# A later planned landing for all four query tiles of the opening attention head

## The chip, the core and the metric

The kernel runs on one core of a Trainium2 chip. The metric is the device time of one execution in microseconds, lower is better. The kernel before takes 1893.55 us, the median of three runs (1892.68 to 1895.55).

## The reference

One layer of a streaming encoder. A prompt of 2048 frames and a sample of 64 frames with 4096 cached frames go through the same layer:

```python
h = rmsnorm(x, norm_g) @ w_in          # 1024 -> 6144 columns: qa ka va za qb kb vb zb ga gb
# branch A: differential attention, 4 heads, two 64-wide halves c of q and k, values 128 wide
s = einsum('bqhcd,bkhcd->bhcqk', q, k) * 64 ** -0.5 - slope[h] * abs(q_pos - k_pos)
s = where(k_pos // 64 <= q_pos // 64, s, -inf)
p = softmax(s);  a = p[:, :, 0] - lam * p[:, :, 1];  oa = einsum('bhqk,bkhe->bqhe', a, v)
# branch B: retention, 4 heads, 128-wide keys and values, a decayed state over chunks of 64
# output: x + (sigmoid(ga) * ((rms(oa) * silu(za)) @ w_oa) + sigmoid(gb) * ((rms(ob) * silu(zb)) @ w_ob)) @ w_out
```

It returns both outputs, the normalised keys, the values and the final retention states.

## The kernel before, in words

All products are made in pairs of rounded operands: a high part (`wh`, `xh`, `ath`) and the low rest (`wl`, `xl`, `atl`), and each product takes three matmuls. The projection is streamed in two halves of 1024 frames. Its weights come in slabs of 128 rows of `w_in`: SP loads a slab into `ws` (line 266, three buffers), ACT rounds it to `wh` (line 993), GpSimd subtracts to get `wl` (line 1003), and TensorE uses it (line 1039, tile `mm`). A group of 512 columns needs eight slabs. The value columns of the second half are such a group: one tile of 128 frames takes 24 matmuls of 512 columns, slab by slab, and its result is taken out by ACT as `thi` (line 1287, a single buffer) and `raw` (line 1289), by DVE as `tlo` (line 1291), and stored by SP (line 271).

Attention of the first 1024 frames runs while the projection of the second half goes on. A head has four query tiles, p = 0 to 3, of 256 frames each, here numbered within the half. `load_head` (line 1472) loads a head's keys `K` and values `V`, `load_q` (line 1509) loads a query tile with four transfers of 128 KB into one of two buffers `q`. `attn_head` (line 1550) takes the tiles in turn: for each of a tile's two blocks of 128 queries and each half c it makes scores (lines 1582 and 1583, into banks `s` or `tp`), DVE takes them out with the distance term (line 1591), ACT takes the exponential (line 1622), DVE mixes the two halves (line 1644), TensorE transposes the result (line 1694, tile `at`), ACT and DVE split it into `ath` (line 1708) and `atl` (line 1710), and TensorE multiplies by the values (lines 1672 to 1674, tile `pv`).

Nothing of this order is decided on the chip. A planner in Python runs generators as tasks, keeps an estimated clock for each engine (`self.pe`, `self.act` and so on), and writes down instructions in the order in which the tasks come due. Each engine and SP's queue then work through their own list strictly in order, held by semaphores. A task that yields a time is not resumed before the planner's TensorE clock has reached it; until then tasks of lower rank, above all the projection, put their matmuls into the list. `load_q` puts each tile with the time `t` at which the planner takes it to have landed into the list `self.qs`, and `attn_head` yields that time (`yield tq`) before the tile's scores. So a later `t` puts more projection matmuls ahead of these scores in TensorE's list; it adds no wait to the program. `FIRSTQ` is 4000 of the planner's nanoseconds, and in the kernel before it is added to the first tile (line 1494) alone:

```python
        q, tq = self.qs.pop(0)
        yield tq
```

Of the kernel before, what the change touches and what calls it, by code (L numbers as in the profile page):

```python
# [44 lines left out]
FIRSTQ = 4000.0  # L45
# [118 lines left out]
class Hybrid:  # L164
# [1307 lines left out]
    def load_head(self, half, h):  # L1472
        ap = self.ap
        nu = half + 1
        ks = [[None] * nu for _ in range(2)]
        vs = [[None] * nu for _ in range(2)]
        tk = tv = 0
        for u in range(nu):
            usl = slice(1024 * u, 1024 * u + 1024)
            for c in range(2):  # L1480
                yield from self.take("K")
                k = self.sb(ap, [128, 1024], "K", dt=F32R)
                for j in range(2):
                    o = 64 * (j ^ c)
                    tk = self.ld(k[o:o + 64].bitcast(F32), self.kT[j][h, 64 * c:64 * c + 64, usl], 1 << 18)
                ks[c][u] = k
        hd = {"ks": ks, "vs": vs, "tk": tk, "tv": None}
        if self.far:
            self.heads.append(hd)
        else:  # L1490
            self.far = True
            yield from self.load_q(0, 0)
            q, t = self.qs[0]
            self.qs[0] = q, t + FIRSTQ
            yield self.pe + 3000
            yield from self.load_q(0, 1)
            yield self.pe + 2000
            self.ld(self.dfar, self.i["c_dfar"], 1 << 19)
            self.heads.append(hd)
        for u in range(nu):  # L1500
            usl = slice(1024 * u, 1024 * u + 1024)
            for j in range(2):
                yield from self.take("V")
                v = self.sb(ap, [128, 8, 128], "V", dt=F32R)
                tv = self.ld(v.bitcast(F32), self.vN[j][usl, 128 * h:128 * h + 128]
                             .rearrange("(t p) e -> p t e", p=128), 1 << 19)
                vs[j][u] = v
        hd["tv"] = tv

    def load_q(self, h, p):  # L1510
        t0 = 256 * p
        yield from self.take("q")
        q = self.sb(self.ap, [128, 4, 256], "q", dt=F32R)
        for j in range(2):
            qj = self.qT[j][h, :, t0:t0 + 256].rearrange("(c d) t -> d c t", c=2)
            for o in (0, 64):
                t = self.ld(q[o:o + 64, 2 * j:2 * j + 2].bitcast(F32), qj, 1 << 17)
        self.qs.append((q, t))

    def q_loader(self, half):  # L1520
        for h in range(4):
# [1373 lines left out]
```

## Time and profile before

| | us |
|---|---|
| median of the three runs | 1893.55 |
| the profiled execution | 1897.48 |
| its span, first to last instruction | 1895.5 |
| TensorE busy in the span (share 99%) | 1877.3 |
| VectorE busy (67%) | 1267.2 |
| ScalarE busy (50%) | 955.9 |

The profiled execution took 1897.48 us, 1.98 us more than its span, and lies 3.93 us above the median. TensorE is busy for all but 18.2 us of the span, so the time is the sum of its work and of the few places where it stands still. The share of an engine says how much of the span it worked; where TensorE stands still, the view of waits and the order of time show what ended the pause. Starts are given in microseconds from the start of the span.

### The profile page before, as it was taken

The numbers are of one execution on the slowest core, as the hardware profiler recorded it, in microseconds if no ns is written. First come the engines' busy times: TensorE is split into PE (matmuls) and PEld (weight loads), VectorE is DVE, ScalarE is ACT, GpSimd is POOL, SyncE is SP. The second block draws the span as 40 slices with busy tenths as digits, with TensorE's granted clock in tenths as the row PEclk, the third lists the DMA queues.
The fourth block names the chain that finished last, engine by engine and source line by source line (L and its number), as shares of the span: only waits on it lengthen the run. The fifth ranks groups of instructions, "written<-read, shape, count | busy, mean of one in ns | idle before, by whom it ended". The sixth has DMA issues, their size and how long they took to land.

```text
span 1895.5 us, 32109 instructions
## 1 busy us (share of the span) xinstructions
PE 1877.3 (99%) x10970; PEld 1649.7 (87%) x10970; DVE 1267.2 (67%) x2994; ACT 955.9 (50%) x2217; POOL 590.8 (31%) x557
## 2 busy tenths in 40 slices
PE   9999999999999899999999999999999999999999
PEld 7788888888888789888888899999999999999887
DVE  6765856657575667877577776687873329977664
ACT  6434654454434566455556555566664436654221
POOL 2420356555643132031211112211113526522442
PEclk9999999999999999999999999999999999999999
DMA  7654555565566785565523444734414748876542
GB/s 255 213 175 124 169 169 165 168 193 180 179 181 187 222 233 157 143 204 135 160 73 105 137 120 119 203 85 116 116 52 127 227 133 261 269 237 205 174 157 77
DMA packets 360581, 313.01 MB, mean 165 GB/s; under 512 B 67937, under 2 KB 310241, under 8 KB 360418
## 3 DMA queue, kind: packets, MB, share of 16 engines
q1 hardware_dynamic: 360418, 310.97, 56.0%
q8 instruction: 86, 1.41, 0.3%
q14 instruction: 77, 0.63, 0.1%
HBM read 205.43 MB, written 104.60 MB: 164 GB/s over the span
## 4 chain that ended last, share of the span: by engine, by line
PE 65%; DMA 2%; SPq 1%; DVE 1%; ACT 0%; issue 0%; POOL 0%; DVEq 0%; POOLq 0%; ACTq 0%
PE mm L1039 26%; PE at L1694 3%; PE s L1582 2%; PE s L1583 2%; PE pv L1674 2%; PE pv L1673 2%; PE pv L1672 2%; PE s L2496 1%; PE s L2498 1%; PE s L2497 1%; PE mm L2372 1%; PE at L2373 1%; PE s L2372 1%; PE s L2373 1%; PE at L2372 1%; PE s L2374 1%
## 5 line engine op out<-in xcount | busy, mean ns | idle before, releaser
L1003 POOL TENSOR_TENSOR wl<-ws,wh 128x512 fp32r<-128x512 f32 x125 | 172.5, 1396 | 360.5 <-ACT wh L993 271.8
L1039 PE MATMUL mm<-xh,wh 128*128 128x256 f32 (+2 forms) x784 | 258.4, 330 | 0.0
L1039 PE MATMUL mm<-xh,wl 128*128 128x256 f32 (+2 forms) x784 | 254.4, 324 | 0.0
L1039 PE MATMUL mm<-xl,wh 128*128 128x256 f32 (+2 forms) x784 | 254.2, 324 | 0.0
L1039 PE MATMUL mm<-wh,xh 128*128 128x512 f32 x504 | 203.3, 403 | 0.0
L1039 PE MATMUL mm<-wh,xl 128*128 128x512 f32 x504 | 197.8, 392 | 0.0
L1039 PE MATMUL mm<-wl,xh 128*128 128x512 f32 x504 | 197.6, 392 | 0.0
L1622 ACT ACTIVATE row<-row,a_mx 128x1024 f32<-128x1024 f32 (+7 forms) x144 | 149.6, 1041 | 16.4 <-DVE a_mx L1601 16.4
L1039 PEld LDWEIGHTS mm<-xh,wl 128*128 128x128 f32 x784 | 148.1, 189 | 10.3 <-POOL wl L1003 0.5
L1039 PEld LDWEIGHTS mm<-xh,wh 128*128 128x128 f32 x784 | 148.2, 189 | 9.9
L1039 PEld LDWEIGHTS mm<-xl,wh 128*128 128x128 f32 x784 | 148.4, 189 | 9.6
L1710 DVE TENSOR_TENSOR atl<-at,ath 128x512 fp32r<-128x512 f32 (+1 forms) x144 | 92.5, 659 | 80.4 <-ACT ath L1708 80.0
L1448 POOL TENSOR_TENSOR r_y<-r_y,r_sq 128x256 f32<-128x256 f32 x32 | 27.7, 865 | 360.1 <-DVE r_sq L1445 193.3
L1708 ACT CAST ath<-at 128x512 fp32r<-128x512 f32 (+1 forms) x144 | 79.4, 565 | 105.8 <-PE at L1694 103.5
L1591 DVE CUSTOM_DVE_ANT_0 row<-s,dfar 128x512 f32<-128x512 f32 (+2 forms) x150 | 93.2, 635 | 52.5 <-PE s L1583 47.6
L768 POOL TENSOR_TENSOR wl<-ws,wh 128x256 fp32r<-128x256 f32 x64 | 57.5, 899 | 190.7 <-ACT wh L759 187.1
L1039 PEld LDWEIGHTS mm<-wh,xl 128*128 128x128 f32 x504 | 94.7, 188 | 21.3
L1039 PEld LDWEIGHTS mm<-wh,xh 128*128 128x128 f32 x504 | 94.8, 188 | 17.4 <-DVE tlo L1291 0.2
L1039 PEld LDWEIGHTS mm<-wl,xh 128*128 128x128 f32 x504 | 95.0, 188 | 17.0
L1644 DVE SCALAR_TENSOR_TENSOR row<-row,a_w 128x1024 f32<-128x1024 f32 (+5 forms) x88 | 98.9, 1131 | 0.0
L993 ACT CAST wh<-ws 128x512 fp32r<-128x512 f32 x128 | 76.9, 621 | 38.6 <-DMA ws<-in_w_in_dram 25.8
L1582 PE MATMUL s<-K,q 128*128 128x512 f32 (+3 forms) x244 | 93.2, 384 | 1.3 <-DVE a_acc L1591 1.0
(497 smaller groups left out, 5441.3 us busy)
## 6 DMA issues: line engine op xcount, KB each, us to landing
ws<-in_w_in_dram SPq DMA_DIRECT2D x160, 256.0 KB, 3.5
q<-qT SPq DMA_DIRECT2D x128, 128.0 KB, 3.7
K<-kT SPq DMA_DIRECT2D x48, 256.0 KB, 4.3
V<-vN SPq DMA_DIRECT2D x24, 512.0 KB, 5.2
row<-in_x_prompt_dram SPq DMA_DIRECT2D x16, 512.0 KB, 4.4
wz<-in_w_in_dram SPq DMA_DIRECT2D x32, 256.0 KB, 4.3
row<-in_cache_k_T_dram SPq DMA_DIRECT2D x32, 256.0 KB, 3.5
row<-in_cache_v_diff_dram SPq DMA_DIRECT2D x32, 256.0 KB, 3.1
```

Of the source, the lines that this page charges most:

```text
L768: nc.gpsimd.tensor_sub(l[:, cs], src, h[:, cs].bitcast(F32))
L993: self.nc.scalar.copy(h, st)
L1003: self.nc.gpsimd.tensor_sub(l, st, h.bitcast(F32))
L1039: nc.tensor.matmul(ps, p, q, start=c == 0 and i == 0, stop=c == KC - 1 and i == 2)
L1582: nc.tensor.matmul(ps, q1s, kk, start=True, stop=False)
L1591: nc.vector.tensor_tensor_reduce(out=row[:, k0:k0 + n], in0=ps, in1=tab, scale=-SLOPES[h], scalar=3.0e38, op0=ALU.add, op1=ALU.min, accum_ ...
L1622: nc.scalar.activation(u, u, AF.Exp, bias=mx, scale=-1.0, accum_out=lp[:, k:k + 1])
L1644: nc.vector.scalar_tensor_tensor(out=u0, in0=u1, scalar=w[:, 0:1], in1=u0, op0=ALU.mult, op1=ALU.add)
L1694: nc.tensor.transpose(at[:, w:w + 128], src, self.ident)
L1708: nc.scalar.copy(ah[:, :w], at[:, :w])
L1710: nc.vector.tensor_sub(al[:, :w], at[:, :w], ah[:, :w].bitcast(F32))
L2372: nc.tensor.matmul(ps, wh[:, u, csl], oh, start=kt == 0, stop=False)
```

## The change

`FIRSTQ` is no longer added to the first tile after it has been loaded, but by `load_q` to every tile of head 0 with p up to 3, which are the four tiles of the first half's first head:

```diff
@@ -1490,8 +1490,6 @@
         else:
             self.far = True
             yield from self.load_q(0, 0)
-            q, t = self.qs[0]
-            self.qs[0] = q, t + FIRSTQ
             yield self.pe + 3000
             yield from self.load_q(0, 1)
             yield self.pe + 2000
@@ -1515,7 +1513,7 @@
             qj = self.qT[j][h, :, t0:t0 + 256].rearrange("(c d) t -> d c t", c=2)
             for o in (0, 64):
                 t = self.ld(q[o:o + 64, 2 * j:2 * j + 2].bitcast(F32), qj, 1 << 17)
-        self.qs.append((q, t))
+        self.qs.append((q, t if h or p > 3 else t + FIRSTQ))
```

No instruction is added or taken away; the lists are put in another order from the second query tile on. Lines of the changed kernel after 1494 are numbered two lower (1580 for 1582).

On TensorE, where the second query tile's scores (`q_6284`) begin. Before:

```order
L1583 MATMUL s_6411<-K_6243,q_6246 128x256
L1582 MATMUL s_6418<-K_6240,q_6284 128x384
L1583 MATMUL s_6418<-K_6240,q_6284 128x384
L1582 MATMUL tp_6435<-K_6243,q_6284 128x384
L1583 MATMUL tp_6435<-K_6243,q_6284 128x384
```

and in the changed kernel:

```order
L1581 MATMUL s_6411<-K_6243,q_6246 128x256
L1039 MATMUL mm_6364<-xh1_6086,wh_5993 128x320
L1039 MATMUL mm_6364<-xl1_6087,wh_5993 128x320
L1039 MATMUL mm_6364<-xh1_6086,wl_5994 128x320
L1039 MATMUL mm_6364<-xh1_6086,wh_5993 128x320
L1039 MATMUL mm_6364<-xl1_6087,wh_5993 128x320
L1039 MATMUL mm_6364<-xh1_6086,wl_5994 128x320
L1039 MATMUL mm_6443<-wh_6017,xh0_6021 128x512
L1039 MATMUL mm_6443<-wl_6018,xh0_6021 128x512
L1039 MATMUL mm_6443<-wh_6017,xl0_6022 128x512
L1580 MATMUL s_6453<-K_6240,q_6284 128x384
```

Nine projection matmuls now stand between the first tile's last score and the second tile's first.

Still on TensorE, where the third query tile (`q_6428`, in the changed kernel `q_6426`) begins, in the first frame tile of the value columns (`mm_6476`, now `mm_6443`). Before, with five of the eight slabs used:

```order
L1039 MATMUL mm_6476<-wh_6374,xh0_6021 128x512
L1039 MATMUL mm_6476<-wl_6375,xh0_6021 128x512
L1039 MATMUL mm_6476<-wh_6374,xl0_6022 128x512
L1582 MATMUL tp_6511<-K_6240,q_6428 128x256
L1583 MATMUL tp_6511<-K_6240,q_6428 128x256
L1582 MATMUL s_6515<-K_6240,q_6428 128x384
```

and in the changed kernel, the sixth slab to the eighth and the start of the next frame tile; three transposes and six more projection matmuls lie between the last row shown here and the third query tile:

```order
L1039 MATMUL mm_6443<-wh_6385,xh0_6021 128x512
L1039 MATMUL mm_6443<-wl_6386,xh0_6021 128x512
L1039 MATMUL mm_6443<-wh_6385,xl0_6022 128x512
L1039 MATMUL mm_6443<-wh_6422,xh0_6021 128x512
L1039 MATMUL mm_6443<-wl_6423,xh0_6021 128x512
L1039 MATMUL mm_6443<-wh_6422,xl0_6022 128x512
L1039 MATMUL mm_6443<-wh_6449,xh0_6021 128x512
L1039 MATMUL mm_6443<-wl_6450,xh0_6021 128x512
L1039 MATMUL mm_6443<-wh_6449,xl0_6022 128x512
L1039 MATMUL mm_6533<-wh_6017,xh0_6021 128x512
L1039 MATMUL mm_6533<-wl_6018,xh0_6021 128x512
L1039 MATMUL mm_6533<-wh_6017,xl0_6022 128x512
```

The first frame tile's last slab (`wh_6449`, before `wh_6482`) used to come after the third query tile's first six score matmuls and now comes ahead of them; the third query tile stands behind 18 more projection matmuls and three transposes.

On ACT, around the second frame tile's result (`thi_6667`, now `thi_6660`) and the second query tile's transposed result (`ath_6678`, now `ath_6671`). Before:

```order
L1622 ACTIVATE row_6222,a_lp_6638<-row_6222,a_mx_6590 128x768
L1287 CAST thi_6667<-mm_6593 128x512
L1289 COPY raw_6666<-mm_6593 128x512
L1708 CAST ath_6678<-at_6673 128x512
L1708 CAST ath_6686<-at_6682 128x384
```

and in the changed kernel:

```order
L1620 ACTIVATE row_6222,a_lp_6635<-row_6222,a_mx_6613 128x640
L1287 CAST thi_6660<-mm_6533 128x512
L1289 COPY raw_6659<-mm_6533 128x512
L1706 CAST ath_6671<-at_6666 128x512
L1706 CAST ath_6679<-at_6675 128x384
```

The two casts of the attention result stand behind the value result's cast in both; one exponential has moved behind them. On SP's queue the loads and stores from the first query tile's load to the second frame tile's value stores come in one order in both kernels, apart from two small stores that go one place ahead, past one weight load. Five loads later the two orders part.

## The prediction

> **What bounds the kernel now.** I read the page first: does one engine set the time, and how long does it stand still?
>
> ```profile
> span 1895.5 us, 32109 instructions
> PE 1877.3 (99%) x10970; PEld 1649.7 (87%) x10970; DVE 1267.2 (67%) x2994; ACT 955.9 (50%) x2217; POOL 590.8 (31%) x557
> ```
>
> TensorE (PE) does. The change neither adds nor removes work, so it can only move the 18.2 us in which PE is idle. The busy time by stretches (columns: stretch, its length, busy time and instructions of PE, PEld, DVE, ACT, POOL, granted clock, DMA share, GB/s) tells where those lie:
>
> ```profile
> 596.00:640.00 44.00, 36.97 (x221) 32.62 (x220) 17.14 (x64) 18.79 (x48) 7.64 (x6) 0.99 1.00 260
> 640.00:700.00 60.00, 59.12 (x357) 52.11 (x357) 40.05 (x120) 35.16 (x90) 12.39 (x10) 0.98 0.74 215
> 700.00:1450.00 750.00, 747.86 (x4805) 678.72 (x4804) 543.43 (x1529) 427.25 (x952) 138.07 (x112) 1.00 0.46 129
> ```
>
> 7.0 us lie in the 44 us in which the opening head starts, and there the DMA engines are busy throughout (share 1.00). In the 810 us behind, PE idles 0.88 + 2.14 = 3.0 us. The view of PE's waits names the two large ones (total, count, longest):
>
> ```profile
> PE pv L1672 <- ACT ath L1708: 2.7, 1, 2.7
> PE tp L1582 <- DMA q<-qT: 2.6, 1, 2.6
> ```
>
> The change aims at the second. In order of time on PE (start, duration, instruction, in brackets the idle time before it):
>
> ```profile
> 608.41 0.31 PE L1039 MATMUL mm<-xh,wh 128*128 128x320 f32 x1
> 608.56 0.31 PE L1039 MATMUL mm<-xl,wh 128*128 128x320 f32 x1
> ...
> 608.97 0.28 PE L1583 MATMUL s<-K,q 128*128 128x256 f32 x1
> 609.59 0.41 PE L1582 MATMUL s<-K,q 128*128 128x384 f32 x1 [0.34 <-DMA q<-qT]
> 610.57 0.41 PE L1583 MATMUL s<-K,q 128*128 128x384 f32 x1 [0.57 <-DMA q<-qT]
> 610.82 0.33 PE L1582 MATMUL tp<-K,q 128*128 128x384 f32 x1
> 610.99 0.34 PE L1583 MATMUL tp<-K,q 128*128 128x384 f32 x1
> ...
> 612.97 0.39 PE L1039 MATMUL mm<-wh,xh 128*128 128x512 f32 x1
> ...
> 616.17 0.39 PE L1039 MATMUL mm<-wh,xl 128*128 128x512 f32 x1
> 619.12 0.36 PE L1582 MATMUL tp<-K,q 128*128 128x256 f32 x1 [2.55 <-DMA q<-qT]
> 620.04 0.36 PE L1583 MATMUL tp<-K,q 128*128 128x256 f32 x1 [0.57 <-DMA q<-qT]
> ```
>
> Starts count here, since matmuls overlap. 15 matmuls of 512 columns start from 612.97 to 616.17, so one takes 3.20 / 14 = 0.229 us; one of 320 columns takes 0.15, of 384 0.17, and in proportion one of 256 about 0.12. Beyond these paces the second query tile costs 0.50 + 0.81 us (starts 609.59, 610.57) and the third 2.72 + 0.80 us (619.12, 620.04), together **4.83 us**. The other large wait comes 18 us later, first on PE, then on ACT:
>
> ```profile
> 634.82 0.39 PE L1039 MATMUL mm<-wh,xl 128*128 128x512 f32 x1
> 637.87 0.39 PE L1672 MATMUL pv<-ath,V 128*128 128x256 f32 x1 [2.66 <-ACT ath L1708]
> 638.09 0.28 PE L1673 MATMUL pv<-ath,V 128*128 128x256 f32 x1
> 638.71 0.39 PE L1674 MATMUL pv<-atl,V 128*128 128x256 f32 x1 [0.33 <-DVE atl L1710]
> ```
>
> ```profile
> 636.25 0.58 ACT L1287 CAST thi<-mm 128x512 fp32r<-128x512 f32 x1 [6.00 <-DMA vN<-thi]
> 637.21 0.99 ACT L1708 CAST ath<-at 128x512 fp32r<-128x512 f32 x2
> ```
>
> ACT stands 6.00 us before a value tile's cast, because the single `thi` buffer is still being stored; the attention casts are queued behind it, and PE loses 637.87 - 634.82 - 0.23 = 2.82 us for them and 0.50 more for `atl`. I call this **the gate**.
>
> **The change part by part.**
>
> *The second tile.* PE reaches it at 609.09 now. Nine projection matmuls go ahead: 6 x 0.15 + 3 x 0.23 = 1.57 us, so it starts at 610.66. Its first half was there by 609.59, its second by 610.57: -1.31 us, with 0.1 to 0.3 us to spare.
>
> *The third tile.* It now stands behind 39 projection matmuls instead of 21 since the first tile's scores. Its data are there by 620.04, and whatever else happens PE comes to it after that (below: at 622.9): -3.52 us. Its loads stand at the same place of SP's list and wait for the first tile's last score, which does not move, so I let them land when they do now.
>
> *What is late next.* The last slab of the value weights. SP, ACT and POOL:
>
> ```profile
> 613.51 0.38 SPq L266 DMA_DIRECT2D ws<-in_w_in_dram  x1
> 620.05 0.38 SPq L266 DMA_DIRECT2D ws<-in_w_in_dram  x1
> 624.61 6.04 SPq L266 DMA_DIRECT2D q<-qT  x4
> 630.74 0.54 SPq L271 DMA_DIRECT2D vN<-thi  x1
> ```
>
> ```profile
> 612.01 0.49 ACT L1622 ACTIVATE row<-row,a_acc 128x256 f32<-128x256 f32 x1
> 612.50 0.60 ACT L1622 ACTIVATE row<-row,a_acc 128x384 f32<-128x384 f32 x1
> 616.05 0.43 ACT L1356 COPY ev<-mm 128x320 f32<-128x320 f32 x1 [2.86 <-DMA qbT<-ev]
> 616.37 0.62 ACT L1622 ACTIVATE row<-row,a_acc 128x384 f32<-128x384 f32 x1
> 618.05 0.62 ACT L993 CAST wh<-ws 128x512 fp32r<-128x512 f32 x1 [0.97 <-DMA ws<-in_w_in_dram]
> ```
>
> ```profile
> 618.75 1.27 POOL L1003 TENSOR_TENSOR wl<-ws,wh 128x512 fp32r<-128x512 f32 x1 [5.78 <-ACT wh L993]
> ```
>
> The slab is asked for at 613.51, lands at 618.05, is `wh` at 618.67 and `wl` at 620.02. Now PE uses it after that, behind the third tile. In the new order: second tile from 610.66, six score matmuls to 611.82, three projection matmuls and two more scores to 612.97, then 15 matmuls of slabs three to seven, to 616.40. There `wh` is missing. ACT's order gives no help: the copy that waits to 616.05 now has three exponentials (0.49 + 0.60 + 0.60) between itself and the cast, so the cast starts at about 618.1. PE waits from 616.40 to 618.75, does one matmul, waits from 618.98 to 620.12: 2.35 + 1.14 = **+3.49 us**. Bounds: 0, if the load came 3.5 us sooner, which nothing ahead of it in SP's list would cause; and 4.8, if the busy DMA engines delivered it 1.3 us later. I take 3.49, from the rows. Behind the waiting matmul stand the next frame tile, the first tile's transposes and the third tile's scores (620.12 + 0.46 + 2.06 + 0.24 for the transposes = 622.9).
>
> *The gate.* At this point PE is 4.83 - 3.49 = 1.34 us ahead. Up to the gate the two lists hold the same matmuls. But the gate is not opened by PE: the value store was issued at 630.74 behind the fourth query tile's four transfers (624.61, 6.04 us), these behind the next head's keys and values, and these behind a weight load that waited for POOL's 620.02. All stand in the same order in the changed kernel, in full DMA engines, and start 0.1 us later at most (620.12 for 620.02). So `thi` comes free at 636.2 again and PE goes on at 637.9 again: **+1.34 us** of wait in place of what was won. Bounds: 0, if the store landed 1.34 us or more earlier, and 1.4.
>
> *The clock.* Behind the gate the granted clock is halved:
>
> ```profile
> 639.00:642.30 3.30, 3.30 (x16) 3.12 (x16) 2.82 (x8) 1.22 (x5) 0.73 (x1) 0.50 1.00 313
> ```
>
> 3.30 us at 0.50 cost at least 1.65 us. PE's wait before it grows from 2.66 to about 4.0 us, so I expect the halving again; against the profiled execution that is 0. Whether the timed runs had it the page can't say. Bounds against the median: 0 and +1.65; with nothing to decide, the middle, **+0.8**. The Trainium skill ("TensorE: Matmul & The Clock Gate", section "What's actually happening") has the clock halved after at least one idle window of about 3.4 us, in windows that run freely. The trace shows it after only 2.66 + 0.33 us of idling with two matmuls between, so a full idle window isn't needed here. By the rule a 2.7 us pause would be spared in most runs and a 4 us pause in few, which speaks against the change: the full +1.65.
>
> *The rest of the lists* is shuffled too. Whether later waits shrink or grow I can't read from a trace of before. Bounds: -3.0 us (all idle time up to 1450 us gone) and +5.0 us (one more gate: 2.82 + 0.50 + 1.65). Nearest to the stretch behind, with 3.0 us in 810, is no difference: 0.
>
> **Sum** against the profiled execution: 1897.48 - 4.83 + 3.49 + 1.34 + 0.1 = 1897.6, that is +0.1. The median of the runs lies 3.93 us lower; on it, 1893.55 + 0.1 + 0.8 = **1894.5 us**. What this measurement can tell from no change is about 0.2%, 3.8 us: the forecast is no change.
>
> **The rivals.**
>
> *The gain stays.* The store lands earlier and the slab comes in time, so nothing takes back the 4.83 us: 1893.55 - 4.8 = 1888.7. For it speaks that 4.83 us of waiting for `q` are truly there; against it, that both takers hang on DMA and the DMA share is 1.00. With the slab's wait alone in place, 1892.2.
>
> *A second gate.* The fourth query tile's scores now stand behind the whole third frame tile and the fourth frame tile follows with few rows between; on SP the value stores of these two frame tiles stand back to back. If the third tile's store has not landed when PE is done with the fourth (24 x 0.229 = 5.5 us and some rows later, against the 636.25 - 630.74 = 5.5 us that the store at the gate took), ACT stands before `thi` once more, with attention casts behind it. Price: 5.0 us, 1893.55 + 0.1 + 5.0 = 1898.7; twice, 1903.7. Against it: the DMA share falls to 0.74 behind 640.
>
> *The clock alone.* All as forecast, but the timed runs before were free of the halving and now aren't: 1895.3.
>
> *The change does nothing on the chip.* PE's list is new, but if the loads landed later along with it, the same waits would stand: 1893.6. The unmoved loads on SP speak against it.
>
> **How the numbers follow.** Forecast 0.40, gain stays 0.17, second gate 0.30, clock alone 0.10, nothing 0.03. The shuffled rest spreads each. Faster by over 0.2%: 0.16 from the gain and 0.02 from the forecast, 0.18. Slower: 0.28 from the gate, 0.04 from the forecast, 0.02 from the clock, 0.34. Within: 0.48. The forecast's own range is 1891 to 1897.5, its sum with the rest at -3.0 and +3.0. The range 1888.5 to 1902 takes in the gain and one gate with the clock; about 0.07 is left out below, 0.1 above.
>
> **What would show it.** No `q` among PE's waits near 609 and 619, or under 0.5 us. PE waiting for ACT's `wh` and POOL's `wl` near 616 to 620, 3 to 4 us. ACT waiting for `vN<-thi` to about 636, and PE at the gate for 4 us instead of 2.7, going on at 637.9. A clock of 0.50 behind it. Idle time behind 640 near 3 us; 8 or more would be the second gate. The prediction is wrong in its core if PE passes the gate more than 1 us before 637.9, and in its remainder if the shuffled lists behind it change the idle time by over 3 us.

## The result, and the profile after

| kernel | median, us | range, us | runs |
|---|---|---|---|
| before | 1894.16 | 1892.68 to 1895.81 | 8 |
| changed | 1900.46 | 1896.56 to 1903.34 | 8 |

The ratio is 1.0033 (95% interval 1.0021 to 1.0044): the changed kernel is 6 us slower. On a second chip (the first experiment) it was 1.0020 (1.0011 to 1.0029), 4 us. The forecast of 1894.5 us lay 6 us below the median; the range, 1888.5 to 1902, holds the median. The likeliest case, no difference that can be told, did not come: it is slower by 0.2 to 0.3%.

The profiled execution of the changed kernel took 1899.28 us, 1.2 below its median; that of the kernel before lay 3.3 above its own. So the two traces differ by 1.8 us where the medians differ by 6.3. That will matter below. The page after, its span and busy times:

```profile
span 1897.5 us, 32094 instructions
PE 1878.7 (99%) x10970; PEld 1649.7 (87%) x10970; DVE 1272.4 (67%) x2994; ACT 955.9 (50%) x2217; POOL 585.2 (31%) x557
```

TensorE (PE) is idle for 18.8 us, 0.6 more than before. The stretches (length, busy time of PE, PEld, DVE, ACT, POOL, granted clock, DMA share, GB/s) tell where:

```profile
596.00:640.00 44.00, 39.51 (x231) 34.68 (x230) 17.24 (x66) 18.76 (x48) 7.99 (x7) 0.96 1.03 265
640.00:700.00 60.00, 59.33 (x351) 51.63 (x350) 42.62 (x117) 34.79 (x88) 14.95 (x12) 1.00 0.71 215
700.00:1450.00 750.00, 745.84 (x4802) 676.25 (x4801) 546.71 (x1528) 427.53 (x954) 133.57 (x109) 1.00 0.46 127
```

Around the opening idle time fell from 7.03 to 4.49 us; from 700 to 1450 it rose from 2.14 to 4.16. PE's waits by releaser (total, count, longest):

```profile
PE mm L1039 <- POOL wl L1003: 3.4, 2, 2.5
PE mm L1039 <- ACT wh L993: 2.1, 1, 2.1
PE pv L1670 <- ACT ath L1706: 1.4, 2, 1.1
PE pv L2110 <- DVE row L2104: 1.1, 1, 1.1
PE s L1580 <- DMA q<-qT: 0.9, 1, 0.9
PE s L1581 <- DMA q<-qT: 0.7, 1, 0.7
```

The opening's two query waits are gone; the `q` waits that are left belong to a later head. In order of time on PE, the slab wait and the gate:

```profile
618.51 0.50 PE L1039 MATMUL mm<-wh,xh 128*128 128x512 f32 x1 [2.12 <-ACT wh L993]
620.00 0.51 PE L1039 MATMUL mm<-wl,xh 128*128 128x512 f32 x1 [0.99 <-POOL wl L1003]
...
636.47 0.39 PE L1670 MATMUL pv<-ath,V 128*128 128x256 f32 x1 [1.06 <-ACT ath L1706]
```

The last value slab is missing where the forecast had it missing (618.75 and 620.12). The gate opens 1.4 us earlier than before, and PE waits 1.06 us there, not 2.66. Farther behind, PE stands at places where the first trace of before shows no wait. On PE, SP and GpSimd:

```profile
846.28 0.41 PE L1580 MATMUL s<-K,q 128*128 128x384 f32 x1 [0.86 <-DMA q<-qT]
847.39 0.41 PE L1581 MATMUL s<-K,q 128*128 128x384 f32 x1 [0.69 <-DMA q<-qT]
...
1499.65 0.50 PE L1039 MATMUL mm<-xh,wl 128*128 128x512 f32 x1 [2.46 <-POOL wl L1003]
```

```profile
840.53 1.85 SPq L271 DMA_DIRECT2D obT<-row  x4
842.47 5.18 SPq L266 DMA_DIRECT2D q<-qT  x8
```

```profile
1497.08 1.29 POOL L2310 TENSOR_TENSOR on<-on,z 128x528 f32<-128x528 f32 x1 [1.83 <-DMA on<-obT]
1498.34 3.76 POOL L1003 TENSOR_TENSOR wl<-ws,wh 128x512 fp32r<-128x512 f32 x3
```

The query tile of 846 us is issued behind four retention stores (`obT`), and the slab of 1499 us stands on GpSimd behind a product (`on`) that waits for its own transfer.

For the whole list I use one measure: the time from a matmul's start to the next one's, less the median of that line and shape, where it exceeds 0.2 us. By it PE loses, from 560 to 645 us and behind, 8.4 + 3.8 us before and 5.6 + 8.7 us in the changed kernel. It leaves out a halved clock, at which a matmul of 512 columns takes 0.42 us instead of 0.23 (641.78 to 642.20 in the first trace of before). My first theory was therefore that the opening gains, as it was meant to, and the rearranged rest costs.

### The profile page after: what moved, and what is told of

It reads as the page before. It is cut to its first block, busy times and chain, and to the rows that moved or that the text cites. A ratio compares the mean times of both kernels' runs of the same rounds, so it can differ in the third digit from the quotient of the medians.

```text
span 1897.5 us, 32094 instructions
## 1 busy us (share of the span) xinstructions
PE 1878.7 (99%) x10970; PEld 1649.7 (87%) x10970; DVE 1272.4 (67%) x2994; ACT 955.9 (50%) x2217; POOL 585.2 (31%) x557
## 4 chain that ended last, share of the span: by engine, by line
PE 92%; DMA 3%; DVE 2%; ACT 1%; POOL 1%; issue 1%; SPq 1%; POOLq 0%; ACTq 0%; DVEq 0%
PE mm L1039 33%; PE mm L889 9%; PE tp L889 5%; PE at L1692 3%; PE s L1580 2%; PE s L1581 2%; PE s L889 2%; PE pv L1672 2%; PE pv L1671 2%; PE pv L1670 2%; PE s L2494 1%; PE s L2496 1%; PE s L2495 1%; PE pv L1958 1%; PE s L2370 1%; PE mm L2370 1%
## 5 line engine op out<-in xcount | busy, mean ns | idle before, releaser
L1003 POOL TENSOR_TENSOR wl<-ws,wh 128x512 fp32r<-128x512 f32 x125 | 168.6, 1365 | 304.9 <-ACT wh L993 226.3
L1039 PEld LDWEIGHTS mm<-wl,xh 128*128 128x128 f32 x504 | 95.4, 189 | 18.8 <-POOL wl L1003 1.3
```

Source lines behind the costliest of these rows:

```text
L1003: self.nc.gpsimd.tensor_sub(l, st, h.bitcast(F32))
L1039: nc.tensor.matmul(ps, p, q, start=c == 0 and i == 0, stop=c == KC - 1 and i == 2)
```

## The experiments

Nothing is left out of the computation in any of them. The kernel before was timed beside each group on the same chip; ratios are against it.

**Both kernels once more.** No edit.

> The changed kernel once more, for a second trace and more times beside its hybrids. Theory 1 (the opening itself gains, the rearranged rest of the lists costs more): about 1900 us, 6 above the kernel before; in the trace TensorE again loses about 3.5 us at the last value slab near 619 us and about 1 us at the gate near 636.5, and the later losses (833, 846, 1499 in the first trace) come back in part at the same places. Theory 2 (the opening itself costs and the first trace showed a lucky execution of it): the same time, but this trace loses 5 us or more in the opening (600 to 700 us), for instance at the gate or to a halved clock, and less than 4 us behind 700.

Measured: 1896.33 us (11 runs), before 1892.54 (15): 1.0020 (1.0011 to 1.0029). By the measure above this trace loses 4.9 us in the opening and 6.0 behind it, again near 833, 846 and 1496 us. It waits at the slab, and not at the gate; PE and then ACT:

```profile
617.90 0.50 PE L1039 MATMUL mm<-wh,xh 128*128 128x512 f32 x1 [2.39 <-ACT wh L993]
619.44 0.79 PE L1039 MATMUL mm<-wl,xh 128*128 128x512 f32 x1 [1.04 <-POOL wl L1003]
...
635.83 0.28 PE L1670 MATMUL pv<-ath,V 128*128 128x256 f32 x1
```

```profile
633.99 0.59 ACT L1287 CAST thi<-mm 128x512 fp32r<-128x512 f32 x1 [2.81 <-PE tp L1423]
```

ACT's cast is released here by PE and no longer by the store. So the gate isn't shut in every execution, and a second trace of the kernel before is needed too:

> The kernel before, unchanged, for a second trace beside the first one, whose execution lay 3.3 us above the median. All theories: its own median within 0.5 us. In the trace, if the first one was only a slow execution of the same waits: the waits for the second and third query tile (4.8 us together) and the gate (2.8) come back, and about 3 us are missing elsewhere; if those waits themselves are smaller here, the opening of the kernel before costs less than the prediction took from the first trace.

Measured: 1892.97 us (10 runs), ratio 0.9998 (0.9989 to 1.0007); the profiled execution took 1892.49. PE and ACT:

```profile
618.34 0.36 PE L1582 MATMUL tp<-K,q 128*128 128x256 f32 x1 [2.55 <-DMA q<-qT]
619.73 0.35 PE L1583 MATMUL tp<-K,q 128*128 128x256 f32 x1 [1.03 <-DMA q<-qT]
...
636.33 0.28 PE L1672 MATMUL pv<-ath,V 128*128 128x256 f32 x1
```

```profile
634.38 0.59 ACT L1287 CAST thi<-mm 128x512 fp32r<-128x512 f32 x1 [2.86 <-DMA vN<-thi]
```

The query waits are as large as in the first trace (5.4 us start to start), but the store lands 1.9 us earlier, PE comes 1.1 us later, held up by a halved clock from 620.1 to 623.5 us, and it passes the gate without a wait. This trace loses 5.7 + 2.8 us. Second trace against second trace, the change wins 5.7 - 4.9 = 0.8 us of waits in the opening, but its clock is halved there for 6.8 us (618.6 to 625.4) and that of before for 3.4. One stretch in both, before and changed (the granted clock is the third number from the end):

```profile
622.00:626.00 4.00, 4.00 (x19) 3.19 (x19) 1.82 (x8) 1.45 (x4) 0.00 (x0) 0.81 1.01 224
```

```profile
622.00:626.00 4.00, 4.00 (x16) 3.42 (x15) 2.25 (x9) 0.48 (x1) 0.00 (x0) 0.57 0.98 219
```

The surest measure of the opening is the time from its first score matmul to the first matmul behind the gate's products, between which the two lists hold the same matmuls: 31.36 us before and 31.27 us in the changed kernel. So in this pair the opening gives 0.1 us, and what follows takes 3.7 us longer; the two executions differ by 3.3 us, 0.3 us having been gained ahead of the opening. In the first pair the opening takes 33.26 and 31.09 us, and what follows takes 4.3 us longer.

**Opening and rest exchanged, first attempt.** The planner runs one kernel's rule up to a given matmul; from there its loop takes the tasks in the order that was written down from the other kernel:

```diff
-            w = next(best.gen, "end")
-            if w == "end":
-                self.tasks.remove(best)
-            else:
-                best.wake = w
+            self.step(best)
+            if self.npe >= SWITCH:
+                self.replay()
```

New opening, old rest:

> The changed kernel's opening (all four query tiles of the opening head in its order, through TensorE's row of about 655 us), and behind it every engine's list in the order of the kernel before. Theory 1: the opening's gain alone is left, by the two traces 8.1 - 5.6 = 2.6 us, so 1891.6 us (1890.5 to 1893), below the kernel before. Theory 2: the loss is in the opening, so 1899 to 1901 us, as the changed kernel. Theory 3 (a gate of the kind of the value result's single buffer comes a second time): also above 1897, with TensorE standing 8 us or more between 630 and 700 us.

Old opening, new rest:

> The opening of the kernel before, and behind about 660 us every engine's list in the order of the changed kernel. Theory 1: the cost of the rearranged rest alone, 4.8 us by the two traces (3.8 lost behind 645 us before, 8.65 in the changed kernel) and 6.3 + 2.6 = 8.9 by the medians: 1899 to 1903 us. Theory 2: 1893 to 1895.5 us, as the kernel before.

The control, old and old:

> A control: the order of the kernel before, written out in the way the two hybrids are (opening and rest both old; some 76 of its 9668 TensorE rows still stand a few places off). Both theories: the time of the kernel before within 1 us. If it is off by more, the few places that the way of writing moves cost something themselves, and the hybrids are to be read against this one.

Measured: 1906.89, 1915.58 and 1911.81 us, ratios 1.0078 (1.0066 to 1.0091), 1.0123 (1.0110 to 1.0137) and 1.0100 (1.0086 to 1.0113). The control is 19 us off, so nothing can be read from the times of the two hybrids. The attempt failed, but the control itself says something: 76 of 9668 rows of PE's list a few places off, with what this brought about on the other lists and in the placing of the row buffers, cost 19 us. One of its waits, on PE:

```profile
793.33 0.55 PE L2138 MATMUL at<-row 128*128 128x128 f32 x1 [6.03 <-DMA row<-vbN]
```

Up to 650 us every list of these three is row for row that of the kernel whose opening it has. So the traces show four executions of each opening, and the gate is shut in the control too (PE):

```profile
636.62 0.39 PE L1747 MATMUL pv<-ath,V 128*128 128x256 f32 x1 [2.29 <-ACT ath L1783]
```

**Opening and rest exchanged, second attempt.** The written order now also holds where each row buffer and each bank was placed and the planner's clocks, and only the opening's projection work is moved. From 672 us on, the lists of both hybrids are row for row those of the kernel whose rest they have. No control was run.

```diff
+            if at and (k not in self.ended and (t is None or (t.n, t.m) < (n, m))):
+                self.pe, self.act, self.dve, self.pool, self.dma, _ = at
+            advance(rec[0])
```

> The kernel before in which only the projection matmuls (and the casts and stores of their operands and results) of the opening are moved as the change moves them; the rest of every list is in the old order to the row (TensorE's list is the old one again from row 2790 of 9668, about 660 us, ACT's, DVE's and SP's within the same stretch). Theory 1 (the opening itself gains, the rearranged rest costs): 2.6 us below the kernel before, by the two first traces (8.1 lost in the opening before, 5.6 in the changed kernel); 1 to 3.5 below. Theory 2 (the opening itself costs): 3 to 6 us above, as the changed kernel.

> The changed kernel in which the opening's projection matmuls are put back behind the second and third query tile's scores, as they stood before; behind about 660 us every list is in the changed kernel's order to the row. Theory 1: the cost of the rearranged rest, 4.8 us by the two first traces and up to 8 by the medians (3.8 above on the second chip plus the 2.6 that the opening gains): 4 to 8 us above the kernel before. Theory 2: within 1 us of the kernel before.

Measured: 1896.45 us (11 runs), 1.0017 (1.0008 to 1.0026), and 1904.61 us (5 runs), 1.0060 (1.0046 to 1.0074). Theory 1 falls: the new opening alone does not gain 2.6 us, it costs 3. The trace shows where. The opening takes 31.36 us, as in the second trace of before (it isn't quite the changed kernel's opening: ACT's list parts from that at 611 us, SP's at 614). From 640 to 700 us PE now is idle 2.6 us, where that trace has 0.9; the stretch in this kernel and in that trace:

```profile
640.00:700.00 60.00, 57.43 (x346) 49.34 (x345) 39.04 (x115) 34.94 (x90) 11.20 (x9) 1.00 0.73 214
```

```profile
640.00:700.00 60.00, 59.12 (x365) 52.01 (x364) 41.18 (x124) 38.24 (x97) 14.90 (x12) 1.00 0.76 220
```

The slab wait and the largest piece behind 640, in the retention's chain (PE, first kernel):

```profile
618.68 0.79 PE L1156 MATMUL mm<-wh,xh 128*128 128x512 f32 x1 [2.79 <-ACT wh L1110]
620.22 0.79 PE L1156 MATMUL mm<-wl,xh 128*128 128x512 f32 x1 [0.75 <-POOL wl L1120]
...
652.90 0.39 PE L1539 MATMUL tp<-r_hi,ones 128*128 128x256 f32 x1 [0.95 <-DVE r_hi L1531]
```

With the projection matmuls moved ahead, attention and retention follow each other with less between them, and, as I read these waits, small steps of DVE and ACT are no longer covered. The second hybrid has such joints too (2.08 us at 615.05 for a `row` of DVE, 2.10 at 640.91 for `r_lo`), so its 11 us aren't the cost of the rest alone. A list and its opening can't be priced apart: what one costs depends on the other. Of theory 2 this leaves "the opening gains nothing"; that it alone costs the 4 to 6 us isn't shown.

**The gate in the kernel before.** SP issues the value tile's three stores ahead of the fourth query tile:

```diff
-                t = self.ld(q[o:o + 64, 2 * j:2 * j + 2].bitcast(F32), qj, 1 << 17)
+                dst = q[o:o + 64, 2 * j:2 * j + 2].bitcast(F32)
+                if h == 0 and p == 3:
+                    self.behind.append((dst, qj))
...
+            while self.behind:
+                nc.sync.dma_start(*self.behind.pop(0))
```

> The kernel before with one edit on SP's queue: the four transfers of the opening head's fourth query tile are issued behind the first value tile's three stores, not ahead of them; no other list moves. The prediction's account of the gate (ACT's cast of the attention result waits behind the next value result, that for the store of the single buffer, and that store stands behind the four query transfers): the store is issued 5 us earlier, ACT's 6.0 us wait at 636 goes to near 0 and TensorE's 2.8 + 0.5 us at 637.9 with it, 2 to 4 us below the kernel before unless the later query tile or the lists behind take it back. If the store is slow to land whatever stands ahead of it, or ACT waits for something else, the time is the same.

Measured: 1893.14 us (11 runs), 0.9997 (0.9988 to 1.0006): no difference. SP:

```profile
622.72 1.40 SPq L267 DMA_DIRECT2D V<-vN  x2
624.30 4.02 SPq L272 DMA_DIRECT2D vN<-thi  x1
```

PE does not wait at the gate here, and the opening takes 29.3 us in this trace, where it took 33.3 and 31.4. The timed runs show none of these 2 to 4 us, though the interval leaves room for 2.3; whether the rest of the list takes them back is not shown. And the store was out only 2 to 3 us earlier (at 628.3 us; 630.3 and 631.3 in the traces of before), not 5: this one store stood 4.02 us in issue, at the place where the four query transfers had stood 6.04, of which the first alone took 4.09. So these are not what holds the queue. For the 4.0 us the view of waits names an operation of ACT that the store doesn't need; ahead of both lie the next head's keys and values, 2 MB. In the first hybrid above the store goes ahead of them (SP):

```profile
622.09 0.34 SPq L382 DMA_DIRECT2D vN<-thi  x1
```

There it lands 2.1 us later, ACT's cast does not wait for it, and the first query transfer behind the loads is held instead (3.05 us). In all 13 traces that tell it, the issue that stands right behind these loads goes out 0.15 to 0.49 us before the fourth load of the keys has landed. A queue that was full of them would do that; the fullness itself is not shown.

**The waits taken from the changed kernel.** First the slab: its load goes ahead of four stores on SP, and its cast ahead of a copy and three exponentials on ACT. In the written order the picks of the task that casts the slab move ahead of that copy; the stores:

```diff
+        if self.wloads == WAIT and not grouped:
+            return self.st_late(dst, ev, t0, n, npr)
...
                     self.wst.append((st, t, tag))
                     self.wloads += 1
+                    while self.lateq:
+                        self.nc.sync.dma_start(*self.lateq.pop(0))
```

> The changed kernel with the last value slab made early: its load is issued ahead of four stores of the previous columns on SP (5 us earlier), and its cast stands on ACT ahead of one evacuation and three exponentials; TensorE's, DVE's and GpSimd's lists are untouched. Theory 4 (in the opening the slab wait, 2.55 + 1.31 us in the second trace and 0.7 us of halved clock behind it, takes back what the query waits gave, and the rest of the lists costs the difference to the kernel before): the slab wait goes, 3.5 to 4.6 us off the changed kernel's time, which was 3.8 above the kernel before on a second chip: within 1 us of the kernel before. Theory 5 (what is gained in the opening is given back at later waits, since attention's and the retention's chains are fed no earlier): 1.5 us off at most, 2 or more above the kernel before, with waits near 637 to 700 us that were not there.

Measured: 1900.90 us (5 runs), 1.0038 (1.0026 to 1.0051), no better than the changed kernel. SP, ACT and PE:

```profile
608.47 3.16 SPq L377 DMA_DIRECT2D ws<-in_w_in_dram  x1
```

```profile
616.15 0.62 ACT L1113 CAST wh<-ws 128x512 fp32r<-128x512 f32 x1 [4.38 <-DMA ws<-in_w_in_dram]
634.95 0.58 ACT L1407 CAST thi<-mm 128x512 fp32r<-128x512 f32 x1 [7.51 <-DMA vN<-thi]
```

```profile
616.82 0.50 PE L1159 MATMUL mm<-wh,xh 128*128 128x512 f32 x1 [0.78 <-ACT wh L1113]
618.17 0.49 PE L1159 MATMUL mm<-wl,xh 128*128 128x512 f32 x1 [0.85 <-POOL wl L1123]
...
636.57 0.39 PE L1798 MATMUL pv<-ath,V 128*128 128x256 f32 x1 [4.31 <-ACT ath L1834]
```

The load was held 3.16 us in issue and the cast came 1.1 us earlier only; the slab wait fell from 3.9 us (second trace) to 2.1 us. PE then stood 4.31 us at the gate and went on at 636.57, where the first trace of the changed kernel has 636.47. What was gained ahead of the gate was waited away at it. Theory 4's sum falls; theory 5 is borne out.

The later waits: the query tile ahead of the retention stores, and one slab's low part on DVE.

```diff
+        elif n == 123:
+            self.nc.vector.tensor_sub(l, st, h.bitcast(F32))
+            t = self.G(512, t)
...
-                t = self.st(d3[:, g0, c0:c0 + 128], rh, 1 << 16)
+                if t0 == 896:
+                    self.behind.append((d3[:, g0, c0:c0 + 128], rh))
```

> The changed kernel with two of its later waits taken away: the query tile for which TensorE waits at 844 and 846 us is loaded ahead of the four retention stores (SP's list), and the low part of the weight slab for which it waits at 1496 us is made by DVE and not by GpSimd behind the gate product. Theory 4: 1.9 and 0.8 us in the second trace, so 2.7 off: 1 to 2 us above the kernel before, and the two waits gone from the trace. Theory 5: the same two waits gone but less than 1 us off.

Measured: 1895.96 us (11 runs), 1.0009 (1.0000 to 1.0018), by the ratio 1.7 us above before (2.6 by the medians): as theory 4 said, though the interval overlaps the changed kernel's on the second chip, 1.0011 to 1.0029. The wait near 846 is down to 0.27 us, the one near 1496 is gone, and PE loses 4.3 us behind 645 where the changed kernel lost 6.0 and 8.7. Its gate, though, with lists that are the changed kernel's up to there:

```profile
636.96 0.39 PE L1676 MATMUL pv<-ath,V 128*128 128x256 f32 x1 [3.93 <-ACT ath L1712]
```

Both:

> Both edits of the two runs above in the changed kernel. Theory 4: the two add up, 6 to 7 us off, 2.5 to 3.5 us below the kernel before, faster than both. Theory 5: 2 us off at most, still above the kernel before.

Measured: 1897.83 us (10 runs), 1.0022 (1.0013 to 1.0032): the two don't add up. PE waits 4.37 us at the gate and goes on at 636.15. Behind it the clock is halved for 6.6 us (stretches, the columns as above):

```profile
632.00:636.40 4.40, 0.25 (x2) 0.25 (x2) 0.76 (x2) 1.86 (x5) 0.00 (x0) 1.00 0.90 312
636.60:643.20 6.60, 6.28 (x22) 5.36 (x22) 3.74 (x12) 2.83 (x7) 1.24 (x1) 0.50 1.04 321
```

The last run adds the stores' edit of the gate to both:

> The run with both edits, and a third: on SP the four transfers of the opening head's fourth query tile go behind the first value tile's three stores, so that the single-buffered value result is free some 6 us earlier. Theory 6 (the gate opens at an hour of its own, 635 to 637 us, set by that store and not by TensorE, so that what TensorE gains ahead of it is waited away there; in the run with both edits it stood 4.5 + 0.5 us and 0.6 of halved clock behind it): those 5.5 us go, 1892 to 1893 us, 0.5 to 2 below the kernel before, and in the trace ACT's wait for the store is under 2 us and TensorE's at the gate under 0.5. Theory 5 in its wider form (whatever is freed is waited away at some next place behind 640 us): TensorE's wait at the gate goes, but the time falls by less than 2 us and stays above the kernel before.

Measured: 1893.69 us (11 runs), before 1894.27 (15), 0.9996 (0.9987 to 1.0005). Against the run with both edits the ratio falls by 0.0026, 4.9 us, and the time ends 0.6 us below the kernel before, as theory 6 said, though no difference from it can be told. SP, ACT, PE, and the clock behind:

```profile
622.82 4.75 SPq L385 DMA_DIRECT2D vN<-thi  x1
```

```profile
631.93 0.59 ACT L1412 CAST thi<-mm 128x512 fp32r<-128x512 f32 x1 [4.89 <-DMA vN<-thi]
```

```profile
633.55 0.39 PE L1814 MATMUL pv<-ath,V 128*128 128x256 f32 x1 [1.69 <-ACT ath L1850]
```

```profile
634.60:638.00 3.40, 3.40 (x15) 3.12 (x15) 2.48 (x9) 2.22 (x7) 1.10 (x1) 0.50 0.98 305
```

PE's wait at the gate falls by 2.7 us and the halved stretch is half as long, which is another 1.6. ACT still waits 4.89 us, not under 2, and PE 1.69, not under 0.5: the store again stood 4.75 us in issue. So the size is right and half of the step isn't.

The gate in these traces, in us (the first column is the start of the products less the idle time before them; the last is the time of the opening, as measured above; the first four rows have the lists of the kernel before up to there, the next four those of the changed kernel):

| run | PE is ready | ACT's value cast begins | products begin | PE idle | opening |
|---|---|---|---|---|---|
| before, first trace | 635.21 | 636.25 | 637.87 | 2.66 | 33.26 |
| before, second | 636.33 | 634.38 | 636.33 | 0 | 31.36 |
| first attempt, control | 634.33 | 635.00 | 636.62 | 2.29 | 32.42 |
| first attempt, old opening | 634.61 | 635.25 | 636.87 | 2.26 | 33.07 |
| changed, first | 635.41 | 634.85 | 636.47 | 1.06 | 31.09 |
| changed, second | 635.83 | 633.99 | 635.83 | 0 | 31.27 |
| first attempt, new opening | 636.51 | 634.89 | 636.51 | 0 | 31.28 |
| later waits gone | 633.03 | 635.34 | 636.96 | 3.93 | 33.54 |
| slab early | 632.26 | 634.95 | 636.57 | 4.31 | 32.90 |
| both | 631.78 | 634.54 | 636.15 | 4.37 | 32.50 |
| all three | 631.86 | 631.93 | 633.55 | 1.69 | 29.91 |
| before, store first | 634.98 | 632.69 | 634.98 | 0 | 29.31 |

PE is ready over a span of 4.7 us; in the first ten rows the products begin within 2.0 us of each other, at an hour that ACT sets where PE idles and PE itself where it doesn't. Only where the store is issued earlier, in the last two rows, does the cast come earlier. One list gives openings that differ by 2 us and more from one execution to the next; on average the change wins 0.7 us there (32.5 us in the first four rows, 31.8 in the next four).

## Why the prediction came out as it did

- **The query waits** (-1.31 and -3.52 us). Right: both are gone in every trace of the changed kernel. The second trace of before has them at 1.4 and 4.0 us.
- **The slab wait** (+3.49 us, PE on at 618.75 and 620.12). Right: 618.51 and 620.00, 3.5 us beyond the pace in the first trace and 3.9 in the second.
- **The gate** (+1.34 us, "PE goes on at 637.9 again"). The mechanism was right where PE comes to the gate before the store has landed: what PE gains ahead of it is waited away, and only the store's issue moves its hour (both, all three). The hour was wrong. The prediction said that passing the gate more than 1 us before 637.9 would show its core wrong, and PE passed it at 636.47 and 635.83. The failed step is "so `thi` comes free at 636.2 again". The issue did stay, within 0.4 us, where it was said to stay: 630.31 and 629.68 us in the changed kernel, 630.74 and 629.78 before. But the same store took 4.2 to 5.8 us to land in the ten traces with it in its old place, 5.4 in the first trace of before, and in the nine others ACT's cast begins between 633.99 and 635.34. Nor was the queue held by the four query transfers: a single store in their place stood 4.0 and 4.8 us.
- **The sum of the opening** (-4.83 + 3.49 + 1.34 + 0.1, about 0). In the second pair it came out (0.1 us gained), but by luck in its last term: neither trace stands at the gate, and what took back the rest is a clock halved for 3.4 us longer, ahead of the gate, which costs half of that. In the first pair the opening gained 2.2 us. How often the timed runs stand at the gate the traces can't say: three of four do with the old opening, two of four with the new one.
- **The clock** (+0.8 us, as if the timed runs before might be free of it). Halved stretches stand in both kernels. In the second trace of before it lies at 620 to 623 us, ahead of the gate. The forecast 4 us of wait with the halving behind it is seen in three of the edited kernels, one of which (later waits gone) has the changed kernel's lists up to there, but in neither trace of the changed kernel itself. The term isn't supported. The prediction's reading of the rule that it cites was wrong too: that a pause of 4 us would be spared in few runs does not follow from windows of 3.4 us that run freely (worked out in the last section).
- **The rest of the lists** (0, bounds -3.0 and +5.0 us). This is the step that failed by its size. What follows the gate takes 4.3 us longer in the first pair of traces and 3.7 in the second. By the waits, the changed kernel loses 4.8 and 3.1 us more behind 645 us, over 3 us, which the prediction named as the sign of being wrong there, and 0.7 to 2.6 us at a time: a retention row at 833, a query tile behind stores at 846, a slab on GpSimd at 1496. Taking two of them away brought the ratio from 1.0020 and 1.0033 to 1.0009, an interval that overlaps that of 1.0020 alone. The bounds held it; the value of 0, taken from a quiet stretch of the old list, did not.
- **The rivals.** The gain did not stay. There is no second gate; from 640 to 700 us PE is idle 0.7 us. The slowdown that the prediction gave 0.34 came, but not by the mechanism that carried most of it.

The forecast was 6 us short of the first medians, 3 short by the second chip's ratio: about the rest's 3 to 5 us. So the traces show where the loss lies, behind the gate. That the shuffled rest alone, whatever stands ahead of it, costs what the medians differ by is not shown, since the hybrid meant to price it had waits of its own at the joint.

## What to carry to other kernels

Before a wait is removed, look for the next point whose hour is set by something else, here a store of a single buffer; what is gained ahead of it counts for nothing until that point itself moves. In a list of thousands of instructions in a fixed order, moving a few rows can lay new waits all along the rest: the control above, nearly the old order, cost 19 us here, so the unseen rest deserves a positive price, not zero. And a wait read from one profiled execution can be absent from the next one of the same lists, as the gate was; read several before a sum rests on it.

## What the runs showed of the hardware

- An issue on SP mostly takes 0.3 to 0.6 us. Right behind the two value loads it stood 3.2 us (a slab, of which the view of waits puts 0.8 down to its buffer), 4.0 and 4.8 us (one store) or 3.0 to 4.5 us (the first of the query transfers; the others took 0.6 each), whichever stood there. An issue put ahead of its neighbours at such a place gained 1 to 3 us, not the 5 to 6 that the order promised.
- The halved clock lasted 3.4 us or twice that (all three, both). The Trainium skill ("TensorE: Matmul & The Clock Gate", section "What's actually happening") names a window of 3413 ns, and the lengths agree. It also asks for an idle window of that length; here the halving came after 1.69 + 0.33 us of idling, and not after 1.06 + 0.33 us. By that rule, with windows that run freely, a pause of 2.7 us would never hold a whole window, and one of 4.0 us would in only (4.0 - 3.4) / 3.4, about one run of six (an estimate). As I read the table, its place mattered more than whether it came: at 620 us, ahead of the gate, the slower matmuls filled time that PE would have waited at the gate (ready at 635.4 to 636.5 in the four traces of the table with it there, at 631.8 to 635.2 in the eight without).
- Some of DVE's small operations were slow beside GpSimd's splits, which may be how the row of 833 us came to be late. This was seen, not tested. The changed kernel's GpSimd and DVE:

```profile
820.93 3.92 POOL L1003 TENSOR_TENSOR wl<-ws,wh 128x512 fp32r<-128x512 f32 x3 [1.94 <-DMA ws<-in_w_in_dram]
828.95 2.58 POOL L1003 TENSOR_TENSOR wl<-ws,wh 128x512 fp32r<-128x512 f32 x2 [4.10 <-ACT wh L993]
```

```profile
822.44 1.20 DVE L1224 TENSOR_SCALAR ms<-ms 128x8 f32<-128x8 f32 x1
828.95 1.42 DVE L1414 CAST r_hi<-r_sq 1x256 fp32r<-1x256 f32 x1
```

In this trace the same operation of the same size took 0.17 us in all 12 cases without GpSimd at work and 0.31 to 1.20 us in the four wholly beside it, the cast 0.28 us in 24 cases and 0.87 to 1.42 us in four. Others were not slowed: the reciprocal of line 1631 took 0.16 us in both.
